# Decay sums, modulation rows, rotation and squares leave TensorE's small products; the ordering estimate gets new durations

## The chip, the cores and the metric

The kernel runs on one core of a Trainium2 chip. The metric is the device time of one execution in microseconds, taken as the median of several runs. The core has TensorE (PE; its weight loads are listed apart as PEld), VectorE (DVE), ScalarE (ACT), GpSimd (POOL) and SyncE (SP). They run side by side, each with its instructions in order, and wait for each other through semaphores. Sixteen DMA engines move data between DRAM and the chip's memories.

## The reference

Two layers work on 256 latent and 256 context tokens of width 1024. Each layer modulates its input, runs differential attention and a gated DeltaNet beside each other on it (the token mixer), merges them, and then runs a mixture of 16 experts with two experts for each token. Cut to what the change touches:

```python
m_lat = jnp.split(jax.nn.silu(c) @ mod_w[l] + mod_b[l], 6, axis=-1)      # 12 blocks of 512 columns; the same for c_ctx
...
def rope_2d(x, cos, sin):                       # queries and keys of the attention, latent tokens
    out = jnp.stack([x1 * c - x2 * s, x2 * c + x1 * s], axis=-2)         # halves of 16 channels
...
q = l2_normalize(q.reshape(B, L, G_HEADS, G_KEY_DIM))                     # x * rsqrt(sum(x^2) + eps)
k = l2_normalize(k.reshape(B, L, G_HEADS, G_KEY_DIM))
...
gcum = jnp.cumsum(chunk3(g), axis=-1)
decay = jnp.exp(jnp.where(causal, gcum[..., :, None] - gcum[..., None, :], -jnp.inf))
a_mat = jnp.where(strict, jnp.einsum('nbhid,nbhjd->nbhij', kb, kc) * decay, 0.0)
sol = lax.linalg.triangular_solve(a_mat + jnp.eye(CHUNK), rhs, left_side=True, lower=True, unit_diagonal=True)
qk = jnp.where(causal, jnp.einsum('nbhid,nbhjd->nbhij', qc, kc) * decay, 0.0)
```

## The kernel before

The program is written by a planner while it is built. Each piece of work is a strand (a Python generator) with a priority from the table `PRIO`; every operation that a strand records has a duration estimate for the engine or engines that can do it. The planner (`Scheduler`) keeps a time at which each engine, buffer and DMA is expected to be free, and at each step gives out the operation of the best priority among those that could start first. The order of instructions on every engine, and with it everything that follows, comes from these estimates: `mm`, `mm_beside` and `tr` for TensorE, `dve` for VectorE, `acte` for ScalarE, and a fixed model for DMAs. Nothing of the estimates is in the program itself.

All work lives in a few kinds of buffer: 20 pages of 128x2048 floats, 16 t5 buffers of 128x512, 14 tiny ones and the 8 banks of PSUM. Weights come through the SP queue in one fixed order (`PLAN`), one page at a time, and are split into two parts (`split`) for the three-product form `mm3` of the mixer; the experts' products use plain float32, several experts beside each other (`mm_beside`, line 463). In each layer the token mixer comes first, then the output projection, the routing and the experts. Layer 1 works on the 256 latent tokens wherever the context is not needed (`Y.last`).

The helpers record every operation, so the trace has one line for each helper: products at L451, transposes at L468, two-operand sums and products at L489, three-operand ones (`stt`) at L518, copies at L485, DMAs at L537. Four pieces use TensorE for something small:

- Decay sums. `decay_gates` leaves the running sums `GC`, one column for each of four 128-token tiles t, two directions d and four heads. `grow` makes rows of them: it transposes a column broadcast to 128x128, four heads into one bank. `build` does this for every (t, d) ahead of the capped difference and the exponential, `double` again after its doubling steps, for the tiles whose output is wanted (four in layer 0, two in layer 1).
- Modulation rows. `modulation` makes 12 blocks of 512 columns for each layer; the products of four stretches of the contraction stand beside each other in one bank and still have to be added. For kinds 2 to 5 (eight blocks of each layer) one product with `sel2` adds them, a bias row is added, and the row is stored in `m_dram`, from which `mod_rows` loads it broadcast.
- Rotation. `att_worker` swaps channels with a product by the permutation `perm`, eight times in each layer.
- Squares. `conv_worker` sums squares over the 128 channels with one-column products against `ones`, four for each head of queries and keys (two for layer 1's queries), into the bank `Y.sqb` held until `sq_end`; `norms` reads them there.

```python
def proj_T(Y, b, W, n0, m=128):
    for k in range(8):
        mm3(b[:m, n0:512], [w[:, k, :] for w in W], [x[:, n0:512] for x in hpart(Y, k)], k == 0, k == 7)
```

A float32 product stands in the trace as two matmul instructions with a weight load each; a transpose as one.

## Time and profile before

| | us |
|---|---|
| median of 3 runs (lowest, highest) | 1615.79 (1614.47, 1626.0) |
| the profiled execution's own time | 1628.14 |
| its span, first to last instruction | 1626.0 |
| TensorE busy | 1493.8 |
| TensorE weight loads busy | 1017.6 |
| VectorE busy | 931.7 |
| ScalarE busy | 535.8 |
| moved by DMA | 363.17 MB |

The busy times are those of the profiled execution and overlap each other. Ends of matmuls are modelled, since they are pipelined; the start of the next instruction tells more than a duration does. The mean granted clock of TensorE was 0.954 of full speed.

### The profile page before, as it was taken

How to read it: one execution, taken by the hardware profiler on the slowest of the kernel's cores; microseconds unless marked ns; L12 is line 12 of the kernel's file. 1: busy time of each engine (PE TensorE's matmuls, PEld its weight loads, DVE VectorE, ACT ScalarE, POOL GpSimd, SP SyncE). 2: the span in 40 equal slices, each digit the busy share in tenths (PEclk: the TensorE clock that was granted, in tenths of full speed). 3: DMA queues.
4: the chain of work that ended last, by engine and by line, in shares of the span. 5: the costliest groups of instructions: out<-in, count | busy, mean ns of one | idle time of the engine just before them, and what ended most of it. 6: DMA issues, size and time to landing. Idle time of an engine off the chain costs nothing. (4 is left out here: it accounts for less than half of the span.)

```text
span 1626.0 us, 24829 instructions
## 1 busy us (share of the span) xinstructions
PE 1493.8 (92%) x9551; PEld 1017.6 (63%) x9552; DVE 931.7 (57%) x2391; ACT 535.8 (33%) x950; POOL 63.1 (4%) x84
## 2 busy tenths in 40 slices
PE   5999999999999977999999899999999957999974
PEld 2776788756787843465564367788889844454421
DVE  1677945768437586365575966792778666210023
ACT  2533343434331121264553253343554302110110
POOL 1000000000000001111010000000000000000000
PEclk9999999999999997999998999996999977999988
DMA  9415522152336577799998743440055955899994
GB/s 312 158 53 175 160 57 80 50 210 91 117 130 249 190 302 283 277 422 403 417 383 326 260 151 109 156 102 5 28 182 176 312 218 214 304 421 421 420 408 203
DMA packets 147725, 363.17 MB, mean 223 GB/s; under 512 B 27932, under 2 KB 82284, under 8 KB 122256
## 3 DMA queue, kind: packets, MB, share of 16 engines
q1 hardware_dynamic: 139808, 342.91, 56.9%
q0 software_dynamic: 6512, 16.38, 3.0%
q10 hardware_dynamic: 1280, 2.23, 0.4%
q8 instruction: 77, 1.26, 0.3%
q14 instruction: 48, 0.39, 0.1%
HBM read 345.47 MB, written 21.56 MB: 226 GB/s over the span
## 5 line engine op out<-in xcount | busy, mean ns | idle before, releaser
L451 PE MATMUL bank<-page,page 128*128 128x512 f32 (+3 forms) x3776 | 733.7, 349 | 13.5 <-ACT page L485 6.5
L451 PEld LDWEIGHTS bank<-page,page 128*128 128x128 f32 (+2 forms) x3776 | 567.6, 189 | 126.1 <-issue 27.3
L489 DVE TENSOR_TENSOR page<-page,page 128x1024 fp32r<-128x1024 f32 (+3 forms) x219 | 250.8, 1164 | 96.9 <-ACT page L485 94.9
L485 ACT ACTIVATE page<-page 128x1024 fp32r<-128x1024 f32 (+1 forms) x196 | 200.3, 1046 | 122.8 <-PE bank L451 65.8
L463 PE MATMUL bank<-page,t 128*64 128x512 f32 (+2 forms) x736 | 208.9, 607 | 6.8 <-DMA page<-in_w_exp_dram 5.9
L485 ACT ACTIVATE t<-bank 128x512 f32<-128x512 f32 (+5 forms) x168 | 79.8, 480 | 306.7 <-PE bank L468 210.5
L489 DVE TENSOR_TENSOR t<-bank,t 128x512 f32<-128x512 f32 (+3 forms) x63 | 49.6, 792 | 188.0 <-PE bank L463 153.8
L485 ACT ACTIVATE page<-bank 128x512 f32<-128x512 f32 (+2 forms) x127 | 70.2, 557 | 222.1 <-PE bank L451 97.9
L463 PE MATMUL bank<-page,page 128*32 128x512 f32 (+2 forms) x512 | 136.0, 604 | 8.0 <-DMA page<-in_w_exp_dram 7.6
L463 PEld LDWEIGHTS bank<-page,t 128*64 128x64 f32 (+2 forms) x736 | 64.6, 147 | 103.4 <-issue 87.1
L451 PE MATMUL bank<-t,page 32*32 32x16 f32 (+4 forms) x1472 | 117.1, 244 | 2.1 <-DVE t L504 1.8
L451 PEld LDWEIGHTS bank<-t,page 128*128 128x128 f32 (+3 forms) x1472 | 104.9, 160 | 18.9 <-issue 11.3
L468 PE MATMUL bank<-cf,t 128*128 128x128 f32 (+2 forms) x468 | 79.1, 287 | 36.0 <-DVE t L489 25.9
L468 PEld LDWEIGHTS bank<-cf,t 128*128 128x128 f32 (+2 forms) x468 | 54.8, 144 | 70.6 <-DVE t L489 31.8
L463 PEld LDWEIGHTS bank<-page,page 128*32 128x32 f32 (+2 forms) x512 | 47.0, 144 | 81.2 <-issue 67.1
L451 PE MATMUL bank<-page,csil 128*32 128x512 f32 x384 | 68.0, 678 | 17.2 <-DMA page<-in_mod_w_dram 16.5
L451 PE MATMUL bank<-page,t 128*128 128x512 f32 (+2 forms) x392 | 81.4, 346 | 2.1 <-DVE page L489 1.1
L451 PEld LDWEIGHTS bank<-page,t 128*128 128x128 f32 (+1 forms) x392 | 56.0, 185 | 26.4 <-issue 9.2
L518 DVE SCALAR_TENSOR_TENSOR t<-bank,tiny,t 128x508 f32<-128x508 f32 (+3 forms) x96 | 66.5, 700 | 7.5 <-ACT t L480 6.4
L480 ACT ACTIVATE t<-bank,tiny 128x512 f32<-128x512 f32 (+1 forms) x72 | 44.6, 623 | 53.5 <-PE bank L451 27.8
L480 ACT ACTIVATE page<-page 128x512 f32<-128x512 f32 (+2 forms) x44 | 25.6, 588 | 84.1 <-DVE page L489 48.5
L468 PE MATMUL bank<-cf,page 128*128 128x128 f32 (+1 forms) x248 | 41.7, 305 | 9.9 <-DMA page<-h_dram,cd 8.4
(178 smaller groups left out, 1139.7 us busy)
## 6 DMA issues: line engine op xcount, KB each, us to landing
page<-in_w_exp_dram SPq DMA_DIRECT2D x192, 1024.0 KB
page<-in_mod_w_dram SPq DMA_DIRECT2D x48, 1024.0 KB
page<-in_w_in_dram SPq DMA_DIRECT2D x44, 1024.0 KB
page<-in_w_o_dram SPq DMA_DIRECT2D x8, 1024.0 KB
y_dram<-t POOLq DMA_DIRECT2D x6, 1024.0 KB, 8.3
page<-m_dram SPq DMA_DIRECT2D x12, 512.0 KB
page<-y_dram SPq DMA_DIRECT2D x6, 1024.0 KB
page<-in_w_pb_dram SPq DMA_DIRECT2D x4, 1024.0 KB
```

The source lines that it names most:

```text
L451: lambda: PE.matmul(o, a, b, start=start, stop=stop, skip_group_check=True))], [o], [a, b])
L463: PE.matmul(o, a, b, start=start, stop=stop, skip_group_check=True)
L468: SC.rec([("PE", 0.11, lambda: PE.transpose(o, a, idn))], [o], [a])
L480: SC.rec([("ACT", acte(width(o), in_psum(a)), lambda: S.activation(o, a, f, bias=bias, scale=scale, **k))], aps(o, accum_out), aps(a, bias ...
L485: SC.rec([("ACT", acte(width(o), in_psum(a)), lambda: S.activation(o, a, AF.Copy, bias=0.0, scale=1.0)), ("DVE", dve(width(o), in_psum(a), ...
L489: opts = [("DVE", dve(width(o), in_psum(a) or in_psum(b)), lambda: V.tensor_tensor(out=o, in0=a, in1=b, op=op)), ("POOL", 0.1 + width(o) * ...
L518: lambda: V.scalar_tensor_tensor(o, a, s, b, op0=op0, op1=op1, **k))],
```

## The change

Six edits. The decay sums are transposed once in each layer (32 rows of 128), stored in `gc_dram`, and loaded from there, broadcast over the partitions, straight into the cell of `A` (`sum_rows`, on ScalarE's queue); `build` and the part after the doubling work on them in place. That part becomes a strand of its own, `decayed`. The modulation blocks of kinds 2 to 5 go to DRAM as four partial rows (`mp_dram`) and come back as 16 partitions by 64 columns, where VectorE adds them and the bias; the layout of `m_dram` changes with it. The rotation swaps channels with a shuffle on VectorE. The squares of the four heads are summed by four products beside each other against 32 columns of ones, and the row of each head is picked by a product with `selH`. The durations of the estimate change; `mm_beside` gets a rate argument that keeps its old value. In the diff, lines left out are context and the same replacement of 0.5 by 0.62 in the estimates of `cpy`, `neg`, `ts`, `affine` and `vcopy`.

```diff
@@ -76,7 +76,6 @@
     blk["ident"] = (r == c)
-    blk["perm"] = (r == (c ^ 16))
     f = np.float32
@@ -95,6 +94,7 @@
     blk["selR"] = (q[:, None] == np.arange(16)[None, :])
+    blk["selH"] = (p[:, None] == 32 * np.arange(16)[None, :])
     blk["neg16"] = np.where(q < 16, -1.0, 0.0)[:, None]
@@ -415,9 +415,11 @@
     x_dram = dp.tile([SEQ_LAT, D], F32, name="x_dram")
-    m_dram = dp.tile([2, 2, 6144], F32, name="m_dram")
+    m_dram = dp.tile([2, 12, 2, 512], F32, name="m_dram")
     blk_dram = [dp.tile([128, 256], F32, name=f"blk{i}_dram") for i in range(2)]
     inv_dram = [dp.tile([128, 256], F32, name=f"inv{i}_dram") for i in range(2)]
+    gc_dram = [dp.tile([32, 128], F32, name=f"gc{l}_dram") for l in range(2)]
+    mp_dram = dp.tile([2, 12, 4, 1024], F32, name="mp_dram")
@@ -442,11 +444,11 @@
         n = max(width(b), 16)
-        t = n / 2400 if b.dtype == BF or (b.dtype == F32R and n >= 256) else n / 600
+        t = n / 2250 if b.dtype == BF or (b.dtype == F32R and n >= 256) else n / 600
         if beside:
...
         elif b.dtype == F32:
-            t = max(t, width(a) / 1200)
+            t = max(t, width(a) / 580)
         SC.rec([("PE", max(t, 0.022) + 0.003,
@@ -456,22 +458,22 @@
-    def mm_beside(os, as_, bs, start, stop):
+    def mm_beside(os, as_, bs, start, stop, rate=600):
...
                 PE.matmul(o, a, b, start=start, stop=stop, skip_group_check=True)
-        SC.rec([("PE", width(bs[0]) / 600 + 0.008 * len(os), f)], list(os), [*as_, *bs])
+        SC.rec([("PE", width(bs[0]) / rate + 0.008 * len(os), f)], list(os), [*as_, *bs])
...
         idn = ident if idn is None else idn
-        SC.rec([("PE", 0.11, lambda: PE.transpose(o, a, idn))], [o], [a])
+        SC.rec([("PE", 0.112, lambda: PE.transpose(o, a, idn))], [o], [a])
     def dve(n, ps, r=1.0):
-        return 0.065 + n * 0.00104 * (1.0 if ps else r) + (0.06 if ps else 0.0)
+        return 0.15 + n * 0.00104 * (1.0 if ps else r) + (0.02 if ps else 0.0)
     def acte(n, ps):
-        return (0.05 if ps else 0.093) + n * 0.000834
+        return (0.175 if ps else 0.21) + n * 0.00082
...
@@ -825,30 +827,35 @@
             SC.free(b)
-            b = yield "bank"
             if kind < 2:
+                b = yield "bank"
                 bk = b.v(4, 2)
...
                 tt(modc[:, l, kind, half * 4:half * 4 + 4, :], bk, modb[:, c:c + 4, None].to_broadcast([128, 4, 2]), OP.add)
+                SC.free(b)
             else:
+
                 br_ = yield "t5"
-                br = br_.v(512)[0:2, :]
-                dma(br, dram(mod_b, l * 6144 + i * 512, [[0, 2], [1, 512]]), "ACT")
-                bk = b.v(512)
-                mm(bk[:2, :], K["sel2"], part, True, True)
-                tt(part[:2, :], bk[:2, :], br, OP.add)
-                dma(m_dram[l, :, i * 512:(i + 1) * 512], part[:2, :], "ACT")
+                br, at = br_.v(8, 64)[:16], (l * 12 + i) * 4096
+                for s in range(2):
+                    dma(dram(mp_dram, at + 512 * s, [[1024, 4], [1, 512]]), part[s:128:32, :], "ACT")
+                    dma(br[8 * s:8 * s + 8, 4], dram(mod_b, l * 6144 + i * 512, [[64, 8], [1, 64]]), "ACT")
+                dma(br[:, 0:4], dram(mp_dram, at, [[64, 16], [1024, 4], [1, 64]]), "ACT")
+                tt(br[:, 0:2], br[:, 0:2], br[:, 2:4], OP.add)
+                tt(br[:, 0], br[:, 0], br[:, 1], OP.add)
+                tt(br[:, 0], br[:, 0], br[:, 4], OP.add)
+                dma(dram(m_dram, (l * 12 + i) * 1024, [[64, 16], [1, 64]]), br[:, 0], "ACT")
                 SC.free(br_)
-            SC.free(b, pt_)
+            SC.free(pt_)
             SC.set(mod_ev[(l, i)])
...
         yield mod_ev[(l, 2 * kind + 1)]
-        dma(o, dram(m_dram, (l * 2 + s) * 6144 + kind * 1024, [[0, 128], [1, 1024]]))
+        dma(shaped(o, (2, 512)), dram(m_dram, (l * 24 + 4 * kind + s) * 512, [[0, 128], [1024, 2], [1, 512]]))
@@ -995,8 +1002,7 @@
         Y.rn = Y.gv[:, 12:14, 0:16].rearrange("p k (t h) -> p k t h", t=4)
-        Y.sqb = yield "bank"
-        Y.sqs = Y.sqb.v(2, 4, 4)
+        Y.sq = {}
         SC.set(Y.gdn_ev)
@@ -1032,8 +1038,7 @@
                 act(a4, dst, AF.Square)
-                for t in range(2 * ns):
-                    mm(Y.sqs[:, 1 - part, 2 * s0 + t, hd:hd + 1], a4[:, t, :], ones[:, 0:1], True, True)
+                Y.sq[part, hd] = a_
             else:
@@ -1041,8 +1046,7 @@
                 cpy(Y.vtok[:, :, hd, :], tb.v(4, 128))
-                SC.free(tb)
-            SC.free(a_)
+                SC.free(tb, a_)
             SC.set(Y.conv_ev[part, hd])
@@ -1050,10 +1054,21 @@
             yield Y.conv_ev[part, hd]
-        w, w2 = yield ("tiny", "tiny")
-        o = 8 if Y.last and part == 0 else 0
+
+        b = yield "bank"
+        n0 = 256 if Y.last and part == 0 else 0
+        mm_beside([b.v(512)[32 * hd:32 * hd + 32, n0:] for hd in range(4)], [ones[:, :32]] * 4,
+                  [Y.sq[part, hd].v(512)[:, n0:] for hd in range(4)], True, True)
+        st = yield "t5"
+        cpy(st.v(512)[:, n0:], b.v(512)[:, n0:])
+        SC.free(b, *(Y.sq.pop((part, hd)) for hd in range(4)))
+        w, w2, b = yield ("tiny", "tiny", "bank")
+        o = n0 // 32
         sq, z = w.v(16)[:, o:], w2.v(16)[:, o:]
-        vcopy(sq, Y.sqs[:, 1 - part].rearrange("p a b -> p (a b)")[:, o:])
+        for t in range(n0 // 128, 4):
+            mm(b.v(4, 16)[:, t], st.v(4, 128)[:, t], K["selH"], True, True)
+        vcopy(shaped(sq, (4 - n0 // 128, 4)), b.v(4, 16)[:, n0 // 128:, :4])
+        SC.free(b, st)
         rsqrt(Y.gv[:, 13 - part, o:16], sq, 1.0, z)
@@ -1074,11 +1089,6 @@
-    def sq_end(Y):
-        yield Y.q_ev
-        yield Y.k_norm_ev
-        SC.free(Y.sqb)
-
     def decay_gates(Y):
@@ -1137,6 +1147,11 @@
         SC.free(b)
+        b, rows_ = yield ("bank", "t5")
+        tr(b.v(128)[:32], gv[:, 6, :])
+        cpy(rows_.v(128)[:32], b.v(128)[:32])
+        dma(dram(gc_dram[l], 0, [[128, 32], [1, 128]]), rows_.v(128)[:32], "ACT")
+        SC.free(b, rows_)
         act(EGC, GC, AF.Exp)
@@ -1158,10 +1173,10 @@
-    def grow(Y, b, t, d):
-        for hd in range(4):
-            tr(b.v(4, 128)[:, hd, :], hcol(Y.GC, t, d, hd).to_broadcast([128, 128]))
-        return b.v(4, 128)
+    def sum_rows(Y, t, d):
+
+        dma(cell(Y.pA, t, d).rearrange("p h j -> p (h j)"),
+            dram(gc_dram[Y.l], (t * 8 + d * 4) * 128, [[0, 128], [1, 512]]), "ACT")
@@ -1181,21 +1196,20 @@
         yield Y.pt_ev[si]
+        for d in range(2):
+            sum_rows(Y, t, d)
         yield Y.k_norm_ev
...
         for d in range(2):
-            A = cell(Y.pA, t, d)
-            b = yield "bank"
-            gr = grow(Y, b, t, d)
+            A = gr = cell(Y.pA, t, d)
             for hd in range(4):
...
                     stt(A[:, hd], gr[:, hd], hcol(Y.GC, t, d, hd), capP[:, 1], OP.subtract, OP.min)
-            SC.free(b)
             act(A, A, AF.Exp, scale=-1.0 if d == 0 else 1.0)
@@ -1311,24 +1325,32 @@
             SC.free(b, wt)
-            SC.set(Y.u_ev[t, d])
             Y.di_left[si] -= 1
...
             if t in Y.tiles:
-                for hd in range(4):
-                    yield Y.conv_ev[0, hd]
-                b = yield "bank"
-                gr = grow(Y, b, t, d)
-                for hd in range(4):
-                    stt(A[:, hd], gr[:, hd], hcol(Y.GC, t, d, hd), capP[:, d], OP.subtract, OP.min)
-                SC.free(b)
-                act(A, A, AF.Exp)
-                b = yield "bank"
-                for hd in range(4):
-                    mm(b.v(4, 128)[:, hd], Y.kq(hd)[:, t, 0, :], Y.kq(hd)[:, t, 1, :], True, True)
-                tt(A, A, b.v(4, 128), OP.mult)
-                SC.free(b)
+                sum_rows(Y, t, d)
+            else:
+                SC.set(Y.p_ev[t, d])
+            SC.set(Y.u_ev[t, d])
+
+    def decayed(Y, groups):
+
+        for t, d in groups:
+            if t not in Y.tiles:
+                continue
+            yield Y.u_ev[t, d]
+            for hd in range(4):
+                yield Y.conv_ev[0, hd]
+            A = cell(Y.pA, t, d)
+            for hd in range(4):
+                stt(A[:, hd], A[:, hd], hcol(Y.GC, t, d, hd), capP[:, d], OP.subtract, OP.min)
+            act(A, A, AF.Exp)
+            b = yield "bank"
+            for hd in range(4):
+                mm(b.v(4, 128)[:, hd], Y.kq(hd)[:, t, 0, :], Y.kq(hd)[:, t, 1, :], True, True)
+            tt(A, A, b.v(4, 128), OP.mult)
+            SC.free(b)
             SC.set(Y.p_ev[t, d])
@@ -1519,12 +1541,12 @@
                 lat = dst[:, i, 256 - m0:]
-                b = yield "bank"
-                mm(b.v(256), K["perm"], lat, True, True)
-                tt(tmp.v(256), b.v(256), K["sin"], OP.mult)
-                SC.free(b)
-                tt(lat, lat, K["cos"], OP.mult)
-                tt(lat, lat, tmp.v(256), OP.add)
+
+                SC.rec([("DVE", dve(256, False), lambda o=tmp.v(256), a=lat:
+                         V.stream_shuffle(out=o, in_=a, mask=[c ^ 16 for c in range(32)]))], [tmp.v(256)], [lat])
+                tt(tmp.v(256), tmp.v(256), K["sin"], OP.mult)
+                tt(tmp.v(256, o=256), lat, K["cos"], OP.mult)
+                tt(lat, tmp.v(256, o=256), tmp.v(256), OP.add)
                 SC.free(tmp)
@@ -2473,7 +2495,6 @@
         sp(norms(Y, 0), 4, "normq")
-        sp(sq_end(Y), 2, "sqe")
         sp(chunk_pages(Y), 2.7, "pt")
@@ -2482,6 +2503,8 @@
             sp(double(Y, [(a + 1, 1), (a, 1)]), 2.76 + .02 * si, f"dbl{si}b")
+            for n, o in enumerate(([(a, 0), (a + 1, 0)], [(a + 1, 1), (a, 1)])):
+                SC.spawn(decayed(Y, o), PRIO[f"{Y.l}dbl{si}{'fb'[n]}"] + .01, f"dec{si}{'fb'[n]}")
         for d in R2:
...
         sp(gdn_end(Y), 2, "gdne")
```

## Rows read from the trace of the kernel before

**Rows 1.** The page, second part: busy tenths in 40 slices, and the clock.
```profile
PE   5999999999999977999999899999999957999974
...
PEclk9999999999999997999998999996999977999988
```

**Rows 2.** Windows by stage: busy time and count by engine, clock, DMA share, GB/s.
```profile
81.00:528.00 447.00, 438.62 (x3130) 334.02 (x3129) 285.43 (x805) 165.02 (x331) 8.12 (x14) 1.00 0.38 124
950.00:1320.00 370.00, 361.15 (x3113) 307.14 (x3110) 250.34 (x645) 149.19 (x290) 6.71 (x12) 0.95 0.45 150
...
1320.00:1626.00 306.00, 249.78 (x1089) 109.55 (x1089) 95.64 (x302) 38.59 (x68) 6.98 (x7) 0.90 0.79 321
```

**Rows 3.** TensorE's waits, 81 to 528 us: total, times, longest.
```profile
PE bank L451 <- ACT page L480: 2.2, 2, 1.6
```

**Rows 4.** TensorE's waits, 935 to 1320 us.
```profile
PE bank L451 <- ACT page L485: 3.3, 3, 1.3
```

**Rows 5.** Instructions that read tile cb (the masks): 81 to 528, then 935 to 1320 us.
```profile
L518 DVE SCALAR_TENSOR_TENSOR page<-bank,t,cb x64: 332/344/353, 132.7 to 313.3; 128x128 f32<-128x128 f32 x64
...
L518 DVE SCALAR_TENSOR_TENSOR page<-bank,t,cb x48: 229/344/351, 1045.6 to 1189.1; 128x128 f32<-128x128 f32 x48
```

**Rows 6.** Timeline of the weight loads from 150 us: start, duration.
```profile
150.04 0.59 PEld L468 LDWEIGHTS bank<-cf,t 128*128 128x128 f32 x4
150.60 0.53 PEld L451 LDWEIGHTS bank<-page,page 128*128 128x128 f32 x3
```

**Rows 7.** Timeline of the matmuls, 150 to 165 us.
```profile
151.50 1.06 PE L451 MATMUL bank<-page,csil 128*32 128x512 f32 x8
...
154.78 0.70 PE L451 MATMUL bank<-page,cf 128*128 128x256 f32 x2
155.12 5.38 PE L451 MATMUL bank<-page,page 128*128 128x512 f32 x22
160.44 1.02 PE L451 MATMUL bank<-t,cf 128*2 128x512 f32 x2
161.39 3.92 PE L451 MATMUL bank<-page,page 128*128 128x512 f32 x16
```

**Rows 8.** Products that read tile cf (the constants): 81 to 528, then 935 to 1320 us.
```profile
L451 PE MATMUL bank<-t,cf x20: 179/592/592, 121.9 to 411.9; 128*2 128x512 f32 x16, 128*128 128x16 f32 x4
...
L451 PE MATMUL bank<-t,cf x14: 182/592/593, 964.8 to 1283.6; 128*2 128x512 f32 x10, 128*128 128x16 f32 x4
```

**Rows 9.** Groups by line and shape, VectorE: busy us, mean ns, idle before.
```profile
L489 DVE TENSOR_TENSOR t<-bank,t 2x512 f32<-2x512 f32 x16 | 10.8, 673 | 2.1 <-PE bank L451 1.7 <-DMA t<-in_mod_b_dram 0.4
...
L500 DVE STREAM_TRANSPOSE t<-t 128x128 f32<-128x128 f32 x32 | 9.2, 298 | 1.0 <-DMA t<-inv_dram 0.9
...
L489 DVE TENSOR_TENSOR t<-bank,cf 128x256 f32<-128x256 f32 x16 | 6.7, 419 | 12.2 <-PE bank L451 12.2
```

**Rows 10.** Tile m_dram: issues on ScalarE's queue, ns.
```profile
L537 ACTq DMA_DIRECT2D m_dram<-t x16: 229/230/251, 160.7 to 1288.3; - x16
```

**Rows 11.** Timeline of the weight loads from 58 us.
```profile
60.48 1.05 PEld L451 LDWEIGHTS bank<-ones,t 128*128 128x128 f32 x8
```

**Rows 12.** Windows of 5 us from 1055 to 1095 us: their sum.
```profile
sum 40.00, PE 39.88 PEld 35.52 DVE 38.54 ACT 16.52 POOL 1.77; mean PE 4.99 PEld 4.44 DVE 4.82 ACT 2.06 POOL 0.22
```

**Rows 13.** Windows by slice: the one from 1098 us.
```profile
1098.00:1138.00 40.00, 40.00 (x423) 35.23 (x425) 9.48 (x28) 12.05 (x35) 1.05 (x2) 0.62 0.04 5
```

**Rows 14.** Timeline of all engines from 176 us; idle time before in brackets.
```profile
177.77 0.36 ACTq L537 DMA_DIRECT2D inv_dram<-t  x1
...
178.43 3.93 PE L451 MATMUL bank<-page,page 128*128 128x512 f32 x16
...
179.42 1.06 ACT L485 ACTIVATE page<-page 128x1024 fp32r<-128x1024 f32 x1 [2.32 <-DVE t L529]
...
179.57 1.30 SPq L537 DMA_DIRECT2D t<-inv_dram  x3
```

**Rows 15.** Line 537 (the DMAs), the last line of the answer.
```profile
DMA to landing us min/median/max: 1.8/7.8/12.8
```

More of the change, by code (lines that the diff above doesn't have):

```diff
@@ L485, in cpy @@
         SC.rec([("ACT", acte(width(o), in_psum(a)), lambda: S.activation(o, a, AF.Copy, bias=0.0, scale=1.0)),
-                ("DVE", dve(width(o), in_psum(a), 0.5), lambda: V.tensor_copy(o, a))], [o], [a], pen=1.0)
+                ("DVE", dve(width(o), in_psum(a), 0.62), lambda: V.tensor_copy(o, a))], [o], [a], pen=1.0)
     def tt(o, a, b, op, e="DVE"):
@@ L494, in neg @@
         SC.rec([("ACT", acte(width(o), in_psum(a)), lambda: S.activation(o, a, AF.Copy, bias=0.0, scale=-1.0)),
-                ("DVE", dve(width(o), in_psum(a), 0.5), lambda: V.tensor_scalar(o, a, -1.0, None, op0=OP.mult))],
+                ("DVE", dve(width(o), in_psum(a), 0.62), lambda: V.tensor_scalar(o, a, -1.0, None, op0=OP.mult))],
                [o], [a], pen=1.0)
@@ L521, in vcopy @@
     def vcopy(o, a):
-        SC.rec([("DVE", dve(width(o), in_psum(a), 0.5), lambda: V.tensor_copy(o, a))], [o], [a])
+        SC.rec([("DVE", dve(width(o), in_psum(a), 0.62), lambda: V.tensor_copy(o, a))], [o], [a])
     def vset(o, x, e="DVE"):
```

4 lines of the change are left out of this document (2 added, 2 removed).

## Prediction

> **What bounds the kernel now.** I read the busy tenths by slice first. TensorE stands at 9 in nearly every slice from about 80 to 530 us and again from about 950 to 1320 us; the dips lie between, and the granted clock dips mostly there too [rows 1]. The windows of the two mixer stages (everything ahead of the experts, one stage in each layer) say how full: 438.6 of 447.0 us in layer 0 and 361.2 of 370.0 us in layer 1, with VectorE at 64 and 68% and ScalarE at 37 and 40% [rows 2]. TensorE's own waits, added up over the answer, are 7.6 us in layer 0's stage and 7.9 us in layer 1's; the largest row of each is shown [rows 3, 4]. So in these 817 us nothing is worth much to TensorE but less work for TensorE. From 1320 us on the expert weights bound the kernel (DMA 79% over the window, TensorE 250 of 306 us) [rows 2]: nothing is changed there, and that stage starts when the mixer before it ends. So what a mixer gives back moves the end by as much; what is saved outside the mixers I count at nothing.
>
> **Decay row sums.** Each group is four 128x128 transposes of a broadcast column. VectorE reads one bank per group in four instructions, 64 in layer 0's stage and 48 in layer 1's: 16 and 12 groups [rows 5]. Four weight loads of a group take from 150.04 to 150.60, 0.56 us, and the next work follows at once [rows 6]: 16 x 0.56 = 9.0 us and 12 x 0.56 = 6.7 us go. In comes one transpose per layer (0.14 us) with its eviction and store, and one 256 KB load per group from DRAM. In the build this is issued ahead of the wait for the keys; after the doubling it is issued when the cell of A is free, and the work that reads it moves to a strand of its own, so that the doubling strand goes straight on. The scan waits for that product only at its output step; before it stand products that need no decay, so I put nothing on the path there. 28 x 0.256 MB is 7 MB in stages that use 38 and 45% of the DMA engines [rows 2]: hidden.
>
> **Modulation rows.** The selection product of 512 columns is two instructions, from 160.44 to 161.39: 0.95 us [rows 7]. 16 of the 20 rows of the form in layer 0's stage and 10 of the 14 in layer 1's are such instructions, so 8 and 5 products [rows 8]; the other three lie between the stages and count nothing. 8 x 0.95 = 7.6 us and 5 x 0.95 = 4.8 us. VectorE loses one 0.67 us sum on 2 partitions [rows 9] and gets three narrow ones, about even. ScalarE's queue gets six issues for two, at 0.23 us each [rows 10]: with the row loads some 94 more in all, 22 us on an engine that is idle for two thirds of the span.
>
> **Rotation.** The permutation of 256 columns starts at 154.78 and the next product at 155.12, 0.34 us; half of the 512-column product is 0.48 us [rows 7]. I take 0.41: its own row counts, but ends of products are modelled. Eight in each layer: 3.3 us and 3.3 us. VectorE gets a shuffle that the trace does not have. Its nearest rows are a 128x128 stream transpose at 0.30 us and a 256-column sum at 0.42 us [rows 9]; I take the wider, the width being the same. That is 16 x 0.42 = 6.7 us more on VectorE. (The Trainium skill, VectorE: DVE Perf Modes, "Rules for kernel authors", gives about 2400 ns for a shuffle of 2048 columns at any permutation; my estimate from that page is 0.30 us for 256, 4.8 us in all. No row of this case shows it.)
>
> **Squares.** Eight instructions with one useful column each take 1.05 us [rows 11], mostly weight loads. There is a set for each head of keys and queries, 8 in layer 0 and, the queries being half as long, 6 in layer 1: 8.4 and 6.3 us. In come, per part, four products beside each other (the modulation product has the same form at 1.06 us [rows 7]) and four of 16 columns against a 128-wide stationary (as the old ones: 1.05 us), half of both for layer 1's queries: 2 x 2.11 = 4.2 us and 2.11 + 1.05 = 3.2 us. Net 4.2 and 3.1 us. One PSUM bank is no longer held through the mixer; TensorE hardly waits for banks, so I count nothing. Up to eight t5 buffers are held longer; also nothing, and a reason for the range.
>
> **The estimate.** The durations do nothing on the chip; they decide the order in which the engines get their instructions. In stages where TensorE waits 2% of the time, a better order can return at most those 15.5 us, and a worse one has no bound in the trace. I take 0, and put the ends at 15 us gained and 35 us lost (about what two slow spells, below, cost).
>
> **The sum.** Layer 0: 9.0 + 7.6 + 3.3 + 4.2 - 0.1 = 24.0 us. Layer 1: 6.7 + 4.8 + 3.3 + 3.1 - 0.1 = 17.8 us. Together 41.8 us off TensorE. Against it: from 1055 to 1095 us VectorE is busy 38.5 of 40 us [rows 12], where eight of the build's groups (4.5 us) and most rotations (3.3 us) of layer 1 lie, so up to 7.8 us may not come through; VectorE gets 3.3 us more there from rotations. I take half, 4 us. The other term is ScalarE's queue, 0 to 83 us (second rival); I take 5. Net 41.8 - 4 - 5 = 32.8 us. The profiled execution took 1628.14 us (span 1626.0): 1595.3 us. It lies 12.35 us above the median of the runs, 1615.79, so the forecast is **1583 us**, with 1568 to 1599 as its own range.
>
> **Rivals.** *The clock.* From 1098 to 1138 us the mean granted clock is 0.62 [rows 13]: 30 us of the window at 1.2 GHz and not 2.4, some 15 us lost. Ahead of it TensorE ran the doubling's 32x32 products. The change takes transposes and products out from between the doubling steps, in both layers, so low spells may get longer or more. Against it: layer 0's doubling runs at 1.00 throughout [rows 2], with weight products among it that stay. Two more spells would cost 30 us: 1613 us, no change.
>
> *ScalarE's queue*, the slower side. A load issued there waits in order, and every eviction behind it. The trace shows one: the store of inv_dram issued at 177.77, and ScalarE's next work began at 179.42 after 2.32 idle us; the load of what was stored was issued 1.80 us after the store [rows 14]. After the change 16 modulation read-backs wait for stores on the queue itself, and 28 row loads and 2 stores of sums wait for TensorE or for a store: 46 waits. Queued behind are evictions that free banks for TensorE. At 1.8 us each and all on the path, that is 83 us. For 1.5 us each, 69 us: 1583 - 5 + 69 = 1647 us. It decides (slower by over 1%) from about 1.2 us of TensorE's time per wait. For it: transfers through this line have landed only after 7.8 us at the median and 12.8 at worst [rows 15], though those come from POOL's queue. Against it: TensorE works on through most of that wait [rows 14], and the planner places other ScalarE work ahead of a load that it expects late. The Trainium skill (DMA: Bandwidth & Descriptors, "Queues, rings and completion order") has each DMA engine take turns between the queues by packet, so a small transfer on ScalarE's queue should not stand behind the weights of SP's; by that rule a read-back keeps 1.8 us, 29 us for the 16, and by the POOL rows it would take 7.8, 125 us. No row here shows ScalarE's landings under a full stream.
>
> *The order gives it back.* TensorE has less to do, but the new order makes it wait as much: the priorities stay while every duration under them changes. About 1616 us.
>
> *More than forecast.* The slow spell of layer 1 vanishes and VectorE withholds nothing: 1628.1 - 41.8 - 15 - 12.35 = 1559 us.
>
> **How the numbers follow.** Forecast 0.52, more than forecast 0.12, the clock 0.12, the order 0.08, ScalarE's queue 0.16. About 1% (16 us) is what a measurement of this kernel can tell from no change: faster below 1599.6 us is the first two, 0.64; within 1% the next two, 0.20; slower the last, 0.16. The range reaches from just under the best case to the slower rival's 1.4 us per wait: 1552 to 1640 us.
>
> **What would show it.** Right: 112 transposes fewer, no 2x512 sums, no weight loads against the ones column, TensorE's busy time in the two mixer stages together some 40 us shorter at a similar share, and the expert stages as long as before but earlier. VectorE's sums with the capped masks read a page and not a bank. Wrong on ScalarE: long idle times of ScalarE behind its own DMA issues, with TensorE's waits naming ScalarE. Wrong on the clock: more windows at 0.50. Wrong on layer 1: VectorE at 5.0 in each 5 us while TensorE idles. Most harmful to the forecast would be an order that opens waits of TensorE beyond the 15.5 us of today.

## The result and the profile after

The changed kernel takes 1678.22 us (median of 4 runs, 1669.81 to 1687.19) against 1620.89 for the kernel before: a ratio of 1.034, 95% interval [1.025, 1.044]. The forecast was 1583 us and the range ended at 1640. It went the other way by 57 us, further than the slower rival.

The busy tenths and the granted clock in 40 slices of the kernel after [rows 1]:

```profile
PE   4995999989999896999998799499999975999975
...
PEclk9997998989999897999999899769889986999997
```

A window of the profile gives its length, busy time and count by engine (PE, PEld, DVE, ACT, POOL), clock, DMA share and GB/s. Layer 0's mixer, cut where the stage now ends [rows 2]:

```profile
81.00:557.00 476.00, 433.94 (x3025) 330.92 (x3023) 289.68 (x842) 166.55 (x329) 8.10 (x14) 0.95 0.39 126
```

In layer 0's mixer TensorE was busy for 438.6 of 447 us at full clock; now it is busy for 433.9 of 476 us at 0.95. So 42 us are idle where 8 were, and up to 24 us (5% of 476) went to the lower clock. The products taken out were forecast at 24.0 us; the busy time fell by 4.7, and the lower clock can account for the rest.

From one matmul to another, the same two in both kernels, layer 0's mixer and then layer 1's now read:

```profile
95.10:547.30 452.20, 413.71 (x2928) 314.72 (x2927) 271.27 (x817) 156.29 (x315) 8.10 (x14) 0.94 0.39 125
978.10:1366.30 388.20, 352.00 (x2930) 293.19 (x2931) 257.43 (x690) 148.33 (x290) 6.71 (x12) 0.89 0.45 146
```

In the kernel before they take 422.30 and 361.30 us, with 416.67 and 354.28 us of TensorE (shown below with the decay sums). So with 97 and 92 matmuls less the mixers are 30 and 27 us longer, and TensorE's busy time in them fell by 5 us where the prediction had some 40 as the sign of being right. Over the whole span the mean granted clock fell from 0.954 to 0.924: (1 - 0.954) x 1626.0 = 75 us lost by it before, (1 - 0.924) x 1685.4 = 128 us after, idle time included.

The five longest spells at the lower of the two clock levels (1.2 and 2.4 GHz) in the mixers of the kernel after make 103 us. Two of them lie for the most part in holes of TensorE, which come next. In the other three TensorE is busy nearly throughout:

```profile
269.80:283.60 13.80, 13.70 (x103) 11.73 (x104) 4.93 (x15) 2.94 (x8) 0.52 (x1) 0.51 0.06 20
...
1106.20:1133.60 27.40, 27.40 (x297) 23.28 (x296) 8.64 (x21) 9.26 (x26) 1.05 (x2) 0.50 0.15 41
1208.60:1232.50 23.90, 22.78 (x124) 17.49 (x116) 9.30 (x26) 7.55 (x19) 0.00 (x0) 0.50 0.04 15
```

These are 64 busy us, and up to half of them, 32 us, is what the clock cost there; the mixers before have one long spell, of some 15 us lost [rows 13].

TensorE's longest waits in the two mixer stages (total, times, longest), where no row stood above 2.2 and 3.3 us before [rows 3, 4]:

```profile
PE bank L453 <- ACT page L487: 18.6, 1, 18.6
...
PE bank L470 <- DVE t L520: 23.2, 4, 22.0
```

The timeline around the two, with the idle time before in brackets:

```profile
101.09 4.05 SPq L539 DMA_DIRECT2D page<-in_mod_w_dram  x2
...
141.18 3.79 SPq L539 DMA_DIRECT2D blk_dram<-page  x8
...
149.08 1.30 SPq L539 DMA_DIRECT2D blk_dram<-page  x3
150.48 0.39 SPq L539 DMA_DIRECT2D page<-in_w_in_dram  x1
...
155.79 2.00 ACT L487 ACTIVATE page<-page 128x1024 fp32r<-128x1024 f32 x2 [7.46 <-DMA page<-in_w_in_dram]
...
156.90 1.74 PE L453 MATMUL bank<-page,page 128*128 128x512 f32 x3 [18.58 <-ACT page L487]
...
1087.92 0.35 ACTq L539 DMA_DIRECT2D inv_dram<-t  x1
...
1088.80 0.60 ACT L487 ACTIVATE t<-bank 128x512 f32<-128x512 f32 x1 [15.30 <-DVE t L531]
1089.43 0.50 ACTq L539 DMA_DIRECT2D mp_dram<-t  x1
1089.97 0.48 ACTq L539 DMA_DIRECT2D t<-in_mod_b_dram  x1
1090.49 0.51 ACTq L539 DMA_DIRECT2D mp_dram<-t  x1
1091.04 0.47 ACTq L539 DMA_DIRECT2D t<-in_mod_b_dram  x1
1091.64 0.60 ACT L482 ACTIVATE bank<-t 128x512 f32<-128x512 f32 x1 [2.24 <-DMA t<-in_mod_b_dram]
...
1093.05 0.90 PE L470 MATMUL bank<-cf,t 128*128 128x128 f32 x3 [22.01 <-DVE t L520]
```

Some windows of 5 us in these two holes:

```profile
145.00:150.00 5.00, 0.00 (x0) 0.00 (x0) 4.89 (x23) 1.11 (x2) 0.00 (x0) 0.50 0.15 35
150.00:155.00 5.00, 0.00 (x0) 0.00 (x0) 4.35 (x21) 0.00 (x0) 0.00 (x0) 0.50 0.79 218
155.00:160.00 5.00, 2.97 (x11) 1.02 (x11) 4.16 (x9) 2.00 (x2) 0.00 (x0) 0.50 1.07 298
...
1080.00:1085.00 5.00, 0.00 (x0) 0.00 (x0) 3.72 (x21) 0.00 (x0) 0.52 (x1) 0.50 0.59 146
1085.00:1090.00 5.00, 0.00 (x0) 0.00 (x0) 5.00 (x22) 0.60 (x1) 0.00 (x0) 0.50 1.02 333
```

In both holes TensorE does nothing and VectorE is busy for 74% of a window or more: builds and inversions follow each other there. In layer 0 the wait comes from the order on SP's queue. From 105.14 to 141.18 us it issues nothing, because stores to blk_dram now stand ahead of the weight loads; its waits in this time, and what the kernel before issued in it, are:

```profile
SPq L539 <- DMA page<-gc_dram: 24.9, 1, 24.9
SPq L539 <- DVE page L520: 11.0, 1, 11.0
```

```profile
113.18 7.94 SPq L537 DMA_DIRECT2D page<-in_mod_w_dram  x2
129.34 0.37 SPq L537 DMA_DIRECT2D page<-in_w_in_dram  x1
```

The first store needs a built page, and a build needs its row of sums; yet the builds start no later than before (130.0 against 132.7 us). So the weights, not the builds, are late: the load is issued only at 150.48, ScalarE waits 7.46 us for it before the split, and TensorE stands. In layer 1 the inverse's store stands in ScalarE's queue and ScalarE waits 15.3 us for VectorE, with evictions behind it. When TensorE starts again at 156.9 the clock is still at its lower level.

### The profile page after: what moved, and what is told of

Read it like the earlier page. It is cut to its first block, busy times and chain, and to the rows that moved or that the text cites. A ratio compares the mean times of both kernels' runs of the same rounds, so it can differ in the third digit from the quotient of the medians.

```text
span 1685.4 us, 24575 instructions
## 1 busy us (share of the span) xinstructions
PE 1486.8 (88%) x9325; PEld 1009.9 (60%) x9326; DVE 944.4 (56%) x2478; ACT 527.8 (31%) x933; POOL 64.2 (4%) x84
## 5 line engine op out<-in xcount | busy, mean ns | idle before, releaser
L453 PEld LDWEIGHTS bank<-page,page 128*128 128x128 f32 (+2 forms) x3776 | 568.2, 191 | 148.1 <-issue 32.8
L491 DVE TENSOR_TENSOR page<-page,page 128x1024 fp32r<-128x1024 f32 (+4 forms) x219 | 249.4, 1162 | 109.9 <-ACT page L487 108.1
L487 ACT ACTIVATE page<-page 128x1024 fp32r<-128x1024 f32 (+1 forms) x192 | 195.6, 1046 | 136.5 <-PE bank L453 55.7
L465 PE MATMUL bank<-page,t 128*64 128x512 f32 (+2 forms) x736 | 215.1, 624 | 5.6 <-DMA page<-in_w_exp_dram 4.7
L487 ACT ACTIVATE t<-bank 128x512 f32<-128x512 f32 (+6 forms) x169 | 79.9, 480 | 360.2 <-PE bank L470 200.5
L491 DVE TENSOR_TENSOR t<-bank,t 128x512 f32<-128x512 f32 (+2 forms) x47 | 38.9, 834 | 186.4 <-PE bank L465 152.6
L453 PE MATMUL bank<-t,page 128*128 128x128 f32 (+4 forms) x1472 | 130.0, 254 | 7.1 <-DVE t L502 3.1
L453 PEld LDWEIGHTS bank<-t,page 128*128 128x128 f32 (+3 forms) x1472 | 115.8, 168 | 29.8 <-issue 12.7
L470 PE MATMUL bank<-cf,t 128*128 128x128 f32 (+3 forms) x358 | 63.4, 295 | 49.6 <-DVE t L520 26.5
L453 PE MATMUL bank<-page,csil 128*32 128x512 f32 x384 | 71.3, 713 | 31.5 <-DMA page<-in_mod_w_dram 31.4
L470 PEld LDWEIGHTS bank<-cf,t 128*128 128x128 f32 (+3 forms) x358 | 44.0, 150 | 75.6 <-DVE t L520 23.5
L520 DVE SCALAR_TENSOR_TENSOR t<-bank,tiny,t 128x508 f32<-128x508 f32 (+3 forms) x96 | 65.8, 697 | 12.4 <-ACT t L482 11.2
L491 DVE TENSOR_TENSOR page<-page,bank 128x512 f32<-128x512 f32 x50 | 33.9, 682 | 40.4 <-PE bank L453 34.1
```

What stands on the lines that cost most here:

```text
L453: lambda: PE.matmul(o, a, b, start=start, stop=stop, skip_group_check=True))], [o], [a, b])
L465: PE.matmul(o, a, b, start=start, stop=stop, skip_group_check=True)
L470: SC.rec([("PE", 0.112, lambda: PE.transpose(o, a, idn))], [o], [a])
L487: SC.rec([("ACT", acte(width(o), in_psum(a)), lambda: S.activation(o, a, AF.Copy, bias=0.0, scale=1.0)), ("DVE", dve(width(o), in_psum(a), ...
L491: opts = [("DVE", dve(width(o), in_psum(a) or in_psum(b)), lambda: V.tensor_tensor(out=o, in0=a, in1=b, op=op)), ("POOL", 0.1 + width(o) * ...
L520: lambda: V.scalar_tensor_tensor(o, a, s, b, op0=op0, op1=op1, **k))],
```

## Experiments

Ratios are to the kernel before, run beside it on the same chip; 95% intervals in brackets.

**Durations and work apart.** The first four were to tell three theories apart: (1) the new durations spoil the order under priorities that stayed, (2) without the transposes the builds bunch on VectorE, (3) any new order under the old priorities loses. e1_durations is the kernel before with the change's durations alone, e2_work the reverse:

```diff
-        t = n / 2400 if b.dtype == BF or (b.dtype == F32R and n >= 256) else n / 600
+        t = n / 2250 if b.dtype == BF or (b.dtype == F32R and n >= 256) else n / 600
...
-            t = max(t, width(a) / 1200)
+            t = max(t, width(a) / 580)
```

> The kernel before with the new durations of the estimate alone; the work is that of before. Theory 1, the new durations spoil the order while the priorities stay: 1660 to 1690 us, with waits of TensorE over 10 us that the kernel before does not have. Theory 2, the builds of the decay matrices bunch on VectorE once the transposes are gone, and hold the SP and ScalarE queues: within 10 us of before. Theory 3, any new order under the old priorities loses time, whatever made it new: 1635 to 1690 us.

Measured 1699.7 us, 1.047 [1.041, 1.053]: 79 us lost with the same instructions in another order, more than any of the three theories had named.

> The changed work with the old durations of the estimate. Theory 1 (durations): 1575 to 1595 us, the 33 us of the prediction. Theory 2 (bunching builds): 1655 to 1690 us, with TensorE waiting some 20 us in each layer around the inversion. Theory 3 (any new order): 1610 to 1660 us, 42 us less work and an order that loses more than that.

Measured 1657.87 us, 1.023 [1.018, 1.027]. The work alone, in an order made with the old durations, loses 37 us as well. That lies in the ranges of theories 2 and 3; theory 1 as the only cause falls.

e3_decay has the decay sums alone, with the old durations. e4_nudge has the work of before and one duration moved by 2%:

```diff
-        SC.rec([("PE", 0.11, lambda: PE.transpose(o, a, idn))], [o], [a])
+        SC.rec([("PE", 0.112, lambda: PE.transpose(o, a, idn))], [o], [a])
```

> The kernel before with the decay sums alone taken from TensorE, old durations. Theory 1 (durations): 1600 to 1615 us, 16 us of TensorE less. Theory 2 (bunching builds): 1640 to 1680 us and the long waits of TensorE around the inversions. Theory 3 (any new order): 1630 to 1670 us, with waits in other places than around the inversions.

Measured 1659.59 us, 1.023 [1.018, 1.028], again in the ranges of theories 2 and 3.

> The kernel before with one estimate nudged: a transpose counts 0.112 and not 0.110 us. The work is the same and the estimate as good. Theories 1 and 2: within 10 us of before. Theory 3 (any new order under these priorities loses): 1635 us or more.

Measured 1638.78 us, 1.010 [1.006, 1.014]. A nudge that changes no work costs half of what the decay sums cost: theory 3 had its first support, and the parts had to be tried where the order can't move.

**The parts in the order of the kernel before.** In the h and x runs (and y, below) the planner no longer chooses. A table holds the strand and the engine of every operation and of every buffer grant, in the order of the kernel before:

```diff
-            cand = [(s,) + self.plan(s.q[0]) for s in self.strands if s.q]
...
-            s, o, st = best
+            s = by_num[ORDER[self.step]]
+            e = ORDER[self.step + len(ORDER) // 2]
```

New operations stand behind the one that they follow. The parts' own edits are those of the change's diff.

> The decay sums of the change alone, but every operation is put down in the order that the kernel before has: its order is written into the kernel as a table, the new operations (the transpose, copy and store of the sums' rows, and one read per group) stand right behind the operation that they follow, and no duration is used to choose. Of the 6,779 matmuls, transposes and products that both kernels have, none stands in another order; with the order left to the planner (the run of the decay sums alone, 1.023) 1,160 did. If the order is what was lost (theory 3), this saves about the 15.7 us of the sum less at most the 4 of VectorE: 1605 us, ratio 0.990, and under 1615 in any case. If the work itself is what costs (the rows come late through the DMA queues, and VectorE's row sums from pages hold the builds), it stays where the planner's order had it: 1640 to 1660 us, ratio 1.012 to 1.024.

Measured 1655.42 us, 1.021 [1.016, 1.025]: the second expectation, the work.

> The rotation of the change alone in the order of the kernel before (a table, as in the run of the decay sums): 16 permutation products leave TensorE, 16 shuffles of 256 columns go onto VectorE where the product stood. If the order is what was lost: the 6.6 us of the sum, 1614 us, ratio 0.996. If VectorE's added work is what costs, 16 shuffles of about 0.4 us on VectorE's path: 1621 to 1630 us, ratio 1.000 to 1.006.

Measured 1633.09 us, 1.007 [1.003, 1.011], just above the second expectation. The profiled execution, 1626.21, was the shortest of the six.

> Decay sums, rotation and squares together in the order of the kernel before (20 of 6,707 TensorE operations and 22 of 2,319 on VectorE stand elsewhere, since the norms wait for a page less and a product more). If the order is what was lost: 15.7 + 6.6 + 7.3 less 4 to 9, so 1595 us, ratio 0.984, between 1585 and 1605. If the work is what costs: 1640 us or more, ratio 1.012 or more.

Measured 1667.98 us, 1.029 [1.025, 1.033]: the work again.

> All the work of the change, modulation rows too, in the order of the kernel before (48 of 6,691 TensorE operations stand elsewhere; in the kernel after 2,045 do); durations play no part in the order. If the order is what was lost: the whole sum, 1588 us, ratio 0.980, between 1575 and 1605. If the work is what costs: what it cost with the old durations in the planner's own order, 1650 us, ratio 1.02, or more. In between (1605 to 1635) both have a share, and the run of the three parts against this one says what the modulation rows' three trips through memory take.

Measured 1687.52 us, 1.042 [1.038, 1.046]. So theory 3 as the only cause falls: with the order held the loss is not smaller but larger, 68 us for all the work, where the sum had 32.8 saved. The planner's own order took almost half of that back (e2_work). The held order was made for the old work, so these runs say what the work costs in that order, not in its best one.

**What the decay sums cost, taken apart.** x1_nothing removes the transposes and delivers nothing; x2_kept delivers the rows through memory and makes the transposes too, for nobody; x3_twice is the kernel before with each transpose made twice:

```diff
+            b = yield "bank"
+            grow(Y, b, t, d)
+            SC.free(b)
```

```diff
+            for _ in range(2):
                 tr(b.v(4, 128)[:, hd, :], hcol(Y.GC, t, d, hd).to_broadcast([128, 128]))
```

> The 112 transposes of the decay sums are taken out in the order of the kernel before and nothing takes their place: no row is stored or read, VectorE's subtractions read a constant page (the decay factors are left out of the computation). Theory 6 (late rows: what the held decay run lost are the waits of VectorE and TensorE for rows that come through memory): the saving stays and the waits go, 1621 less 15.7, so 1600 to 1610 us, ratio 0.990. Theory 7 (the clock: the transposes kept TensorE's granted clock up, and without them it falls to its lower level in more stretches): the stretches at 1.2 GHz that the held decay run has at 155 to 260 and 290 to 400 us stay, 1630 to 1650 us, ratio 1.005 to 1.018. Theory 8 (the transposes stood in time that VectorE's chain sets): 1618 to 1624 us, ratio 1.00.

> The held decay run with the 112 transposes put back, into a bank that nobody reads: the rows still come through memory, TensorE does all its old work. Theory 6 (late rows): slower than the held decay run (1655) by the work put back or as slow, 1655 to 1670 us, ratio 1.02 to 1.03. Theory 7 (the clock): the granted clock comes back, and the run is faster than the one with less work, 1625 to 1645 us, ratio 1.003 to 1.015.

> The kernel before in its own order with every transpose of the decay sums made twice, 112 more in the same places. If 0.56 us of a group's four transposes lie on TensorE's path as the sum had it, 28 groups add 15.7 us: 1636 us, ratio 1.010. Theory 7 (the clock): the added columns hold the clock in the stretch at 1098 to 1138 us and so cost less than that, or nothing: 1615 to 1630 us, ratio 0.997 to 1.006. Theory 8 (the time is set by VectorE there): under 1626, ratio 1.00 to 1.003.

Measured: x1_nothing 1770.97 us, which can't be read as a whole, since 142 us come in between 851 and 882 us of before, behind the routing, which sees other numbers here. x2_kept 1654.57 us, 1.021 [1.014, 1.027], as theory 6 had it. x3_twice 1641.51 us, 1.013 [1.007, 1.020], as the sum had it (1.010) and not as theories 7 and 8 did. Since the orders are the same, the same matmul can be looked up in each trace. These windows run from one matmul to another, the same two in each kernel, in layer 0's mixer and then in layer 1's. The kernel before, then h1_decay, x1_nothing, x2_kept and x3_twice:

```profile
96.70:519.00 422.30, 416.67 (x3025) 316.34 (x3024) 265.50 (x769) 154.76 (x317) 8.12 (x14) 1.00 0.39 125
942.80:1304.10 361.30, 354.28 (x3022) 296.30 (x3023) 249.57 (x648) 152.06 (x296) 6.71 (x12) 0.95 0.44 141
```

```profile
98.00:543.00 445.00, 427.19 (x2962) 320.39 (x2962) 265.81 (x770) 154.84 (x317) 8.11 (x14) 0.96 0.39 128
964.60:1331.60 367.00, 353.42 (x2976) 293.62 (x2977) 249.06 (x649) 152.00 (x297) 6.71 (x12) 0.94 0.45 147
```

```profile
97.80:524.10 426.30, 418.20 (x2961) 315.69 (x2960) 264.88 (x768) 155.27 (x317) 8.11 (x14) 0.98 0.39 124
1089.00:1449.00 360.00, 348.92 (x2974) 292.25 (x2975) 248.81 (x648) 151.57 (x296) 6.71 (x12) 0.95 0.44 141
```

```profile
98.20:541.10 442.90, 429.94 (x3027) 324.89 (x3026) 265.69 (x769) 155.07 (x317) 8.11 (x14) 0.97 0.40 128
964.80:1328.10 363.30, 353.65 (x3024) 294.98 (x3024) 249.08 (x649) 152.09 (x297) 6.71 (x12) 0.95 0.46 149
```

```profile
98.50:529.40 430.90, 424.93 (x3089) 324.33 (x3088) 265.83 (x768) 154.97 (x317) 8.12 (x14) 1.00 0.38 122
953.00:1316.50 363.50, 356.40 (x3071) 299.06 (x3072) 249.72 (x649) 152.30 (x296) 6.72 (x12) 0.96 0.43 140
```

Each window is of one profiled execution. How far two executions differ shows in y2_fill (further on), which has in layer 0's mixer the work and the order of the kernel before:

```profile
97.50:523.30 425.80, 418.23 (x3025) 317.35 (x3024) 265.36 (x768) 154.84 (x317) 8.11 (x14) 1.00 0.38 124
```

It takes 3.5 us more, so differences of this size say nothing. Taking 112 transposes out with nothing in their place changes the two stages by +4.0 and -1.3 us: within that, nothing of the 15.7 arrives. TensorE's idle time in the two grows from 12.7 to 19.2 us. In layer 0 TensorE has 64 instructions less and is busy 1.5 us longer, at a clock of 0.98 and not 1.00. Where that goes is seen in a stretch in which TensorE never idles, of the kernel before and of x1_nothing:

```profile
277.10:307.20 30.10, 30.10 (x427) 25.78 (x426) 16.76 (x49) 14.87 (x40) 0.11 (x1) 1.00 0.08 23
```

```profile
276.90:310.70 33.80, 33.80 (x419) 28.66 (x418) 16.79 (x49) 14.92 (x40) 0.14 (x1) 0.85 0.07 20
```

Eight instructions less, full busy time in both, and 3.7 us more at a clock of 0.85. The same stretch in h1_decay and, with the transposes put back, in x2_kept:

```profile
292.80:328.20 35.40, 35.40 (x419) 30.21 (x418) 16.76 (x49) 14.89 (x40) 0.10 (x1) 0.81 0.11 37
```

```profile
297.20:327.40 30.20, 30.20 (x427) 25.87 (x426) 16.92 (x49) 14.93 (x40) 0.17 (x1) 1.00 0.13 41
```

The four kernels of this order without these transposes take 33.5 to 35.4 us here, at 0.81 to 0.90; the eight that have them, the kernel before among them, 30.1 to 31.0 us at 1.00. Making the transposes twice costs 8.6 + 2.2 = 10.8 us. Bringing the rows through memory costs 18.7 + 7.0 = 25.7 us (h1_decay less x1_nothing), or 20.6 + 2.0 with the transposes kept (x2_kept less the kernel before). By the clocks of the windows up to 13 of the 25.7 us are lost at the lower level (h1_decay 17.8 + 22.0, x1_nothing 8.5 + 18.0). VectorE's waits say where: in h1_decay and in x2_kept,

```profile
DVE page L522 <- DMA page<-gc_dram: 24.4, 10, 5.2
```

```profile
DVE page L522 <- DMA page<-gc_dram: 23.3, 11, 5.1
```

So theory 6, late rows, holds for the loss, and theory 7, the clock, for part of the saving that never came; as x2_kept expected it (work put back brings the time back) theory 7 fails for the whole time, since the waits stay, and holds in the stretch just shown.

**Modulation rows, squares, and the clock by itself.**

> The modulation rows of the change alone in the order of the kernel before (17 of 6,875 TensorE operations stand elsewhere): 16 products leave TensorE, 112 transfers through ScalarE's queue and 48 small additions come. The sum had 12.4 us saved: 1609 us, ratio 0.992. If the three trips through memory hold the strand of the modulation, and with it the weights' buffers and the chunks behind: what the run of all parts lost over that of three, 20 us, so 1640 us, ratio 1.012.

Measured 1643.86 us, 1.012 [1.006, 1.019].

```diff
-                dma(br[:, 0:4], dram(mp_dram, at, [[64, 16], [1024, 4], [1, 64]]), "ACT")
+                dma(br[:, 0:4], dram(mp_dram, at, [[64, 16], [1024, 4], [1, 64]]), "POOL")
```

> The run of the modulation rows alone in the order of the kernel before, with the same places for every operation, but the two transfers of a chunk that must wait (the read of the stored partial sums, and the store of the finished row) issued from GpSimd's queue in place of ScalarE's. If ScalarE's queue standing behind them is the cost (11 waits of 2.2 us in the profile of that run): the 20 us go to 0 to 8, so 1621 to 1629 us, ratio 1.000 to 1.005. If it is the additions on VectorE or the rows' later arrival: 1638 to 1650 us, ratio 1.010 to 1.018.

Measured 1635.29 us, 1.008 [1.002, 1.013], between the two, with an interval that overlaps that of h5_modrows. The edit shows the read; the store of the finished row is moved the same way. One of ScalarE's wait rows in h5_modrows:

```profile
ACT page L489 <- DMA mp_dram<-t: 6.5, 3, 2.2
```

All seven such rows make 24.0 us in 11 waits, and 23.7 in 11 with the two transfers moved away. They are not waits for a landing: the timeline of the kernel after shows the four issues ahead of one, 0.50, 0.48, 0.51 and 0.47 us, back to back. ScalarE's time goes into issuing. Whether this is what costs the 20 us isn't shown.

> The squares of the change alone in the order of the kernel before (9 of 6,835 TensorE operations stand elsewhere): 56 one-column products leave, four products that share a pass and 14 small ones come with a copy by ScalarE or VectorE. The sum had 7.3 us saved: 1614 us, ratio 0.996. By difference of the runs of three parts and of the decay sums and rotation alone they cost 3 us: 1624 us, ratio 1.002. If the norms, which now wait for three steps more before the builds can start, hold VectorE's chain: 1630 us or more, ratio 1.005 or more.

Measured 1649.97 us, 1.019 [1.014, 1.024]: the third expectation in its size, and far from the difference of 3. Layer 0's mixer between the same matmuls as above, and a wait of TensorE in it that was 1.8 us in the kernel before:

```profile
97.70:542.10 444.40, 427.66 (x3009) 320.70 (x3008) 265.51 (x768) 155.24 (x318) 8.13 (x14) 0.97 0.36 118
```

```profile
PE bank L455 <- DMA page<-in_mod_w_dram: 9.1, 3, 5.7
```

Of the 22 us more, some 7 are this wait for modulation weights and up to 13 (3% of 444.4) the lower clock. What holds the weights back is not shown. By the ratios the parts held one by one (33, 11, 20 and 30 us) make more than all of them held together (68).

y2_fill puts work in, where the clock is lowest:

```diff
             b = yield "bank"
+            for _ in range(2 * Y.l):
+                tr(b.v(4, 128)[:, 0], ident)
```

> The kernel before in its own order with 64 more transposes, of a constant into a bank that is written over at once: two ahead of each of the four batches of small products in layer 1's doublings, between about 1090 and 1120 us, where the granted clock is 0.50 to 0.62. By the sum's way of counting, work on a busy TensorE: 64 transposes of 0.14 us at 2.4 GHz, some 9 us more, 1630 us, ratio 1.006. If the clock answers to the work that TensorE is given (theory 7): the stretch at 1.2 GHz, worth up to 15 us, gets shorter and pays for them, 1610 to 1621 us, ratio 0.993 to 1.000, and the granted clock of 1100 to 1130 us is over 0.8.

Measured 1635.67 us, 1.009 [1.005, 1.013]. The stretch itself, from one matmul to the same one, first of the kernel before and then of y2_fill:

```profile
1095.90:1136.00 40.10, 39.98 (x423) 34.87 (x422) 8.79 (x25) 13.65 (x41) 1.05 (x2) 0.62 0.05 8
1136.00:1196.30 60.30, 59.89 (x770) 48.05 (x769) 43.63 (x126) 30.86 (x81) 0.99 (x2) 1.00 0.12 37
```

```profile
1099.30:1130.80 31.50, 31.50 (x441) 27.13 (x441) 8.33 (x24) 12.35 (x37) 1.05 (x2) 0.96 0.05 6
1130.80:1194.90 64.10, 63.84 (x801) 51.34 (x800) 43.99 (x126) 30.98 (x81) 0.99 (x2) 1.00 0.11 35
```

With 18 more instructions in it the stretch takes 31.5 us in place of 40.1, and the clock is 0.96 and not 0.62. The fill further on, where the clock was full anyway, costs 3.8 us. Ten other kernels of this order, without the fill, take 37.2 to 40.7 us in the stretch, at 0.59 to 0.68; so theory 7 holds here. The gain shows in this profiled execution (1628.52 us), one of the two shortest; the median of the runs is slower, as the sum's way of counting had it, and their mean clocks (0.949 to 0.962) are no higher than those of the kernel before beside them (0.950 to 0.967). As a version it is worth nothing.

**How good the order of before is.** Two more nudges of the kernel before (the transpose at 0.108; the hand-over at 0.132 in place of 0.130) and one of the changed work (the transpose at 0.112):

> The kernel before with one duration of its planner changed, a transpose from 0.110 to 0.108 us; the same work, 927 of 6,891 TensorE operations in another place. If the order of the kernel before is a chance best (theory 3): 1630 to 1650 us, ratio 1.006 to 1.018, like the first nudge (1.010). If that nudge was a single miss: 1615 to 1626 us, ratio 0.997 to 1.003.

Measured 1665.35 us, 1.026 [1.019, 1.032], beyond theory 3's range.

> The kernel before with one duration of its planner changed, the hand-over between engines from 0.130 to 0.132 us; the same work, 1,103 of 6,891 TensorE operations in another place. Theory 3: 1630 to 1650 us, ratio 1.006 to 1.018. Otherwise 1615 to 1626 us, ratio 0.997 to 1.003.

Measured 1633.45 us, 1.011 [1.005, 1.017], in theory 3's range.

> The changed work with the old durations (1.023) and the transpose at 0.112 in place of 0.110 us: the same work in another order. If that run was an average draw, this comes within 10 us of it: 1648 to 1668 us, ratio 1.017 to 1.029. If it was a bad draw and the work itself is worth the 33 us of the sum against an average order of before (about 1638): 1605 to 1630 us, ratio 0.99 to 1.006.

Measured 1651.73 us, 1.021 [1.016, 1.026]: the first expectation. Three orders drawn anew for the old work cost 18, 46 and 14 us; two for the new work cost 37 and 33. The order of before is the best of four. Between draws no saving by the work shows (26 us lost on average without it, 35 with it), and with a spread of 32 us among three draws a small gain or loss can't be told.

No kernel tried was faster than the kernel before.

## Why the prediction was wrong

*The estimate*, "I take 0", is one of two steps that failed, and its price is twofold. That the order is drawn anew at all costs 14 to 46 us at the same work (three nudges); I had seen one side of it, an order that "opens waits", but not that this kernel's order is the best of those drawn, and that a change of a duration or of work leaves it. The wait in the first hole is of this kind: the new order puts stores ahead of weight loads, and SP's queue stands for 36 us. The new durations come on top: 1.034 against 1.023 and 1.021 for the same work, some 20 us, and 79 us on the old work, 33 beyond the worst nudge; with one order for each, it is not shown that they are worse than another draw. Both together exceed the end of 35 us that I set. The rival *The order gives it back* had this mechanism with a chance of 0.08 and a size that stopped at no change.

*What bounds the kernel now*: "nothing is worth much to TensorE but less work for TensorE" is the other, and with it the sum fell: in the held order, where no duration plays a part, the work that was to save 32.8 us costs 68, and each part alone costs time. A busy share of 98% did not say that the time follows TensorE's work: 15.7 us of transposes removed gave -2.7, the same work added gave 10.8 (20 by the medians). Part of what is freed becomes idle time, 6.5 us in the two mixers, and part, up to 8.5 us in layer 0, is taken by the clock. That VectorE's next step is no earlier would explain the idle time; it was not tested.

*Decay row sums*: "I put nothing on the path there" and "hidden" failed by 25.7 us in the held order; VectorE waits 24.4 us for rows, and the clock falls with it. In the planner's order that wait shrinks to 4.7 us (e3_decay), and the decay sums still cost 37 us. How these 37 divide between late rows and a new draw is not settled: one nudge alone cost more.

*Modulation rows*: their term had the wrong sign, +20 where 12.4 saved were forecast. The issues on ScalarE's queue were costed at 0.23 us each from [rows 10]; those of the new forms take 0.47 to 0.51, four in a row. The rival *ScalarE's queue* had evictions wait behind transfers, 46 times for 1.5 us. In the kernel after the waits of ScalarE behind the transfers of these rows make 14.9 us in 8, hardly for landings; and with the waiting transfers on another queue the part still cost 15 us. What makes up the 20 stays open.

*Rotation*: the shuffle was taken at 0.42 us and takes 0.435; the term is still +11 and not -6.6 in the held order, by the medians. In the traced execution, the shortest, neither mixer is more than 3 us longer than before, so the trace doesn't say which wait it opens.

*Squares*: forecast -7.3, held +30. The trace has the lower clock and the wait for modulation weights; that the new steps (product, copy, product) stand in the way is not shown, and how much of it a free order avoids was not tried.

*The clock* as a rival was right in its mechanism: 53 us more are lost to it than before, where it had 30. It is not only a consequence of holes: some 32 us of the loss in the mixers falls in three spells in which TensorE is busy, where the kernel before has one of 15. In the held order such a spell came when transposes were taken out of a busy stretch and went when they were put back, as the rival had it; how much of the 57 us the clock costs by itself was not separated.

Right were the counts: the 2x512 sums and the 112 weight loads against the ones column are gone, VectorE's masked sums read pages, and the experts take as long as before, only later (the same matmul at 1314.4 us before stands 62 us later, the end 59).

## What to carry to other kernels

When a kernel's order comes from a planner, change one duration in the last digit and time that first: its spread is the least that any change of work must beat, and a tuned order is a draw that the change gives up. A saving counted as work on a busy engine is an upper bound; test it by making the work twice and by taking it out with the order held, and trust only what both show. A transfer in place of a small product puts its latency where the product's consumer stands, and its issue on the queue's engine.

## What the hardware showed that was not expected

TensorE's clock answered here to added work: 0.62 became 0.96 with filling transposes (0.59 to 0.68 in ten more kernels without them), and a stretch with 18 more instructions took 8.6 us less. The Trainium skill (TensorE: Matmul & The Clock Gate, "What's actually happening") has activity release the throttle; the trace agrees with it there. In the other direction it fell from 1.00 to 0.85 in x1_nothing, in a stretch without idle time, where work was only removed, and stood at 1.00 in x2_kept, which has that work again.

Issues of small DMAs on ScalarE's queue (partial rows out, bias in) took 0.47 to 0.51 us each, twice the 0.23 us of [rows 10], and ScalarE executes nothing meanwhile.
